# Values' second parts beside the first in the stationary operand: attention and stick-breaking weights streamed twice instead of three times

## The chip, the cores and the metric

The kernel runs on one core of one Trainium2 chip. The metric is the device time of one execution in microseconds (us), as a median over runs. Five engines matter: TensorE (PE; its loads of the stationary operand are PEld), VectorE (DVE), ScalarE (ACT), GpSimd (POOL), and SyncE (SP), which issues the DMAs.

## What is computed

Two layers of a hybrid trunk over 16 meta tokens and 512 frames, in float32. The first layer has eight heads of sparse attention (an indexer picks the keys) and four heads of gated linear attention; the second has four heads of retention and eight heads of stick-breaking attention. Cut to what the change touches:

```python
# attention, first layer: p is softmax over the chosen keys
return jnp.einsum('bhqk,bqkhd->bqhd', p, vg)
# stick-breaking, second layer
log_1m = jnp.where(ok, -jax.nn.softplus(z), 0.0)
after = lax.cumsum(log_1m, axis=3, reverse=True) - log_1m
w = jnp.where(ok, jnp.exp(jax.nn.log_sigmoid(z) + after), 0.0)
return jnp.einsum('bhqs,bshd->bqhd', w.astype(v.dtype), v)
...
oa = oa.reshape(bsz, P, -1) * jax.nn.silu(ag)
od = od.reshape(bsz, P, -1) * jax.nn.silu(dg)
```

In both, each of eight heads (64 wide) multiplies a matrix of weights, queries by keys, with the values, and the result is multiplied by its gate.

## The kernel before

A product of two float32 matrices is made of three matmuls in the chip's fp32r type: each operand is split into a first part (`hi`, a rounding copy on ScalarE) and a second part (`lo`, the rest, by a subtraction on VectorE), and first x first, second x first and first x second are summed in PSUM. The projections work so (`wh`, `wl` for the weights, `hh`, `hl` for the hidden state, accumulated in `acc`), and so do the sums of values here.

Heads go in pairs, p = 0 to 3 in each layer: `a0` to `a3` in the first (attention), `d0` to `d3` in the second (stick-breaking). `pair` runs a pair by a list of words. `S` makes scores of one head (odd = 0 or 1) for a unit of query blocks (u = 0: blocks 0 and 1; u = 1: blocks 2 and 3), `T` turns the finished weights by transposes into PSUM (`x`) and splits them into `pt` tiles, `M` does the same with the weights on the 16 meta keys (`ptm`), and `P` calls `weighted`, which multiplies the `pt` tiles (moving operand) with the values (stationary operand) into the PSUM tile `y`. There is one `y` buffer; the linear-attention and retention heads use it as well.

Before, one `y` tile of 128 rows x 512 queries belongs to a pair from its first `P` to its end: rows 0 to 63 for the even head, 64 to 127 for the odd one. So that one head's matmul leaves the other's rows alone, the values stand in tiles `vt` (`vh`, `vl`) with 64 zero columns beside each head, cleared on GpSimd: a stationary operand of 128 columns is one head's 64 and 64 zeros. Each key block takes three matmuls (first values x first weights, first x second, second x first), and a pair's end is one VectorE product of `y` with the gate `gt` into the mix `mx`.

The program is recorded first and then put in order by a list scheduler (`Recorder.order`), which gives each instruction a cost and a due time, and takes for each engine what is ready. Every engine then runs its list in that order; buffers of one kind are handed out in the order in which they are first used. All instructions are issued from line 406, so the profile tells them apart by tiles and shapes, not by lines. `out_ab` and `out_cd` are the out-projections; `out_ab` goes over the mix in the order 4, 5, 6, 7, 0, 1, 2, 3, the attention's last pair (`a3`, number 3) at the very end, each part split into `hh` and `hl` by `split_mix`. The first layer's order is `V G0 G1 D A0 A1 C0 C1 A2 A3 C2 C3` (C: the attention's gates), the second's `V S0 S1 R0 S2 S3 R1` (S: stick-breaking, R: retention heads).

## Time and profile before

| | |
|---|---|
| time, median of 3 runs | 653.55 us (652.32 to 654.64) |
| the profiled execution | 654.6 us, of which the span is 652.7 us |
| TensorE busy | 633.3 us (97%), 4469 matmuls |
| VectorE busy | 483.5 us (74%) |
| ScalarE busy | 406.3 us (62%) |
| GpSimd busy | 68.9 us (11%) |

Busy time is the union of an engine's instructions. Matmuls overlap in the engine, so a busy TensorE is not one at its peak, and the duration shown for one matmul is longer than the distance to the next. The profile follows the chain that ended last backward from the end, and says for each idle time which instruction ended it.

### The profile page before, as it was taken

To read this page: it belongs to the slowest core of one execution; us is meant where nothing else is said; L and a number is where in the kernel's file an instruction comes from. 1 tells how busy PE (TensorE), PEld (TensorE's weight loads), DVE (VectorE), ACT (ScalarE), POOL (GpSimd) and SP (SyncE) were. 2 spreads that over 40 slices of the span, in tenths; PEclk is the share of its full clock that TensorE was granted. 3 is DMA by queue.
4 is the path that set the end of the run, shared out by engine and by line. 5 is a ranking of instruction groups with operands and counts; after the bars stand their busy time and mean duration, and the time that the engine had idled before them with its cause. 6 is when DMAs were issued, how large, how long until landed. Compare 5 with 4: busy or idle time off the path is not lost.

```text
span 652.7 us, 12208 instructions
## 1 busy us (share of the span) xinstructions
PE 633.3 (97%) x4469; PEld 582.8 (89%) x4469; DVE 483.5 (74%) x1182; ACT 406.3 (62%) x912; POOL 68.9 (11%) x116
## 2 busy tenths in 40 slices
PE   7999999899999999999999999999999999999995
PEld 6979999898989999999899999888998888988884
DVE  6768799899977859779642674699945699966643
ACT  5656563362344868599643675799844699944434
POOL 4000100120010000001122110001200001110030
PEclk9899999799999999999999999999999999999998
DMA  8437223232322323112243272203322203235403
GB/s 245 111 83 230 66 66 83 58 90 52 80 66 77 89 66 99 50 49 66 65 132 115 65 238 87 66 17 98 82 83 65 77 5 98 65 98 157 150 17 129
DMA packets 91103, 59.25 MB, mean 91 GB/s; under 512 B 7314, under 2 KB 81628, under 8 KB 91044
## 3 DMA queue, kind: packets, MB, share of 16 engines
q1 hardware_dynamic: 91044, 58.48, 31.4%
q8 instruction: 35, 0.57, 0.3%
q14 instruction: 24, 0.20, 0.1%
HBM read 53.18 MB, written 6.90 MB: 92 GB/s over the span
## 4 chain that ended last, share of the span: by engine, by line
PE 78%; DVE 12%; ACT 8%; issue 2%; POOL 0%; DVEq 0%; ACTq 0%; POOLq 0%
PE acc L406 53%; PE x L406 17%; PE y L406 8%; ACT wt L406 4%; DVE st L406 2%; DVE wt L406 2%; DVE wl L406 2%; DVE lt L406 1%; ACT st L406 1%; DVE pt L406 1%; DVE m L406 1%; ACT wh L406 1%; DVE kl L406 1%; ACT ptm L406 1%; ACT pt L406 1%
## 5 line engine op out<-in xcount | busy, mean ns | idle before, releaser
L406 PE MATMUL acc<-hh,wh 128*128 128x272 f32 (+2 forms) x968 | 244.8, 314 | 1.4 <-DVE lt L406 0.4
L406 PE MATMUL acc<-hl,wh 128*128 128x272 f32 (+2 forms) x968 | 236.4, 305 | 0.9 <-DVE hl L406 0.9
L406 PE MATMUL acc<-hh,wl 128*128 128x272 f32 (+2 forms) x968 | 234.6, 303 | 2.1 <-DVE wl L406 2.1
L406 ACT ACTIVATE wh<-raw 128x512 fp32r<-128x512 f32 x154 | 96.1, 631 | 121.5 <-PE acc L406 107.7
L406 PEld LDWEIGHTS acc<-hh,wh 128*128 128x128 f32 x968 | 159.5, 190 | 8.5 <-issue 0.9
L406 PEld LDWEIGHTS acc<-hh,wl 128*128 128x128 f32 x968 | 158.5, 190 | 8.7 <-DVE wl L406 2.9
L406 PEld LDWEIGHTS acc<-hl,wh 128*128 128x128 f32 x968 | 158.6, 190 | 5.4 <-DVE hl L406 1.7
L406 DVE TENSOR_TENSOR wl<-raw,wh 128x512 fp32r<-128x512 f32 x154 | 109.7, 717 | 63.0 <-ACT wh L406 60.7
L406 ACT ACTIVATE wt<-x 128x272 f32<-128x272 f32 (+3 forms) x100 | 43.1, 454 | 24.4 <-PE x L406 15.7
L406 POOL TENSOR_TENSOR gt<-gt,wt 128x528 f32<-128x528 f32 (+1 forms) x16 | 21.7, 1355 | 331.0 <-ACT wt L406 309.7
L406 PE MATMUL x<-st,st 128*128 128x272 f32 (+6 forms) x240 | 50.9, 290 | 0.0
L406 PE MATMUL x<-ident,wt 128*128 128x128 f32 (+2 forms) x300 | 46.0, 274 | 2.0 <-DVE wt L406 1.2
L406 ACT ACTIVATE wt<-wt 128x528 f32<-128x528 f32 (+3 forms) x74 | 43.2, 606 | 3.9 <-DVE wt L406 3.3
L406 PEld LDWEIGHTS x<-st,st 128*128 128x128 f32 (+2 forms) x240 | 37.3, 185 | 7.1 <-ACT wt L406 2.5
L406 ACT ACTIVATE wt<-wt,tiny 128x272 f32<-128x272 f32 (+5 forms) x64 | 34.6, 562 | 9.3 <-DVE tiny L406 8.8
L406 PEld LDWEIGHTS x<-ident,wt 128*128 128x128 f32 (+2 forms) x300 | 34.5, 139 | 6.4 <-DVE pt L406 1.4
L406 PE MATMUL y<-pt,vt 128*128 128x256 f32 (+1 forms) x288 | 39.4, 279 | 0.2 <-DVE pt L406 0.2
L406 PEld LDWEIGHTS y<-pt,vt 128*128 128x128 f32 x288 | 36.6, 190 | 0.9 <-DVE pt L406 0.5
L406 ACT ACTIVATE st<-acc 64x528 fp32r<-64x528 f32 (+1 forms) x58 | 34.7, 599 | 1.0 <-DVE lt L406 0.4
L406 DVE TENSOR_TENSOR_SCAN wt<-wt,wt 128x64 f32<-128x64 f32 (+5 forms) x50 | 30.9, 657 | 2.1 <-ACT wt L406 1.7
L406 ACT ACTIVATE wt<-wt,one 128x528 f32<-128x528 f32 (+3 forms) x42 | 29.5, 704 | 0.2
L406 DVE TENSOR_TENSOR pt<-x,pt 128x384 fp32r<-128x384 f32 (+1 forms) x48 | 28.1, 596 | 1.8 <-ACT pt L406 0.9
(187 smaller groups left out, 884.6 us busy)
## 6 DMA issues: line engine op xcount, KB each, us to landing
raw<-in_w_in_ab_dram SPq DMA_DIRECT2D x64, 256.0 KB, 2.8
raw<-in_w_in_cd_dram SPq DMA_DIRECT2D x56, 256.0 KB, 2.9
raw<-in_w_out_ab_dram SPq DMA_DIRECT2D x16, 256.0 KB, 2.7
raw<-in_w_out_cd_dram SPq DMA_DIRECT2D x16, 256.0 KB, 2.6
rep<-rows SPq DMA_DIRECT2D x8, 328.0 KB, 6.2
lt<-rep SPq DMA_DIRECT2D x8, 264.0 KB, 3.0
pt<-in_x_dram SPq DMA_DIRECT2D x8, 256.0 KB, 4.9
wt<-in_x_dram SPq DMA_DIRECT2D x8, 256.0 KB, 3.1
```

The lines of the kernel that those rows point to most:

```text
L406: getattr(getattr(self.core, o.eng), o.name)(*[bind(x) for x in o.args], **{k: bind(x) for k, x in o.kw.items()})
```

## The change

The zeros go. A tile `vs` holds for each head its first part and its second part side by side, 128 columns, and these are the stationary operand: one pass of the weights' first part gives first x first on one half of the rows and second x first on the other, and a pass of the weights' second part adds to both (second x second comes with it). So each key block takes two matmuls instead of three. The two heads now share all 128 rows and stand in different columns: one `y` tile holds one unit, 256 queries, of both heads, and a pair takes it twice. The values of the meta keys keep their zeros in one tile `vm`; their matmul now runs twice for a unit, once for each head. What the passes leave in the two halves has to be added: `both_parts` copies for each head the half on the other rows to an SBUF tile `low` (ScalarE, 64 x 256) and adds the two halves into `mx` (VectorE, 64 x 256). The product with the gate then works on `mx` in place.

```diff
@@ -457,7 +457,7 @@
         return self.wk.tile([P, 512], dt, tag="pt", bufs=self.PT, name=self.name("pt"))
     def vt(self, dt=F32):
-        return self.wk.tile([P, 768], dt, tag="vt", bufs=8, name=self.name("vt"))
+        return self.wk.tile([P, 1024], dt, tag="vt", bufs=4, name=self.name("vt"))
     def lt(self, dt=F32):
         return self.wk.tile([P, T], dt, tag="lt", bufs=8, name=self.name("lt"))
@@ -968,11 +968,9 @@
         nc = self.nc
-        vh = [self.vt(F32R) for _ in range(NB)]
-        vl = [self.vt(F32R) for _ in range(NB)]
-        vm = self.wk.tile([96, 512], F32R, tag="vm", bufs=1, name=self.name("vm"))
-        for t in vh + vl:
-            nc.gpsimd.memset(t.rearrange("p (f c) -> p f c", f=4)[:, :, 64:128].bitcast(F32), 0.0)
+        vs = [self.vt(F32R) for _ in range(NB)]
+        vm = self.wk.tile([96, 768], F32R, tag="vm", bufs=1, name=self.name("vm"))
+        nc.gpsimd.memset(vm.rearrange("p (f c) -> p f c", f=4)[:, :, 64:128].bitcast(F32), 0.0)
         early = []
         if self.second:
@@ -992,10 +990,10 @@
                 a = self.project(src, col + P * f, self.hh, self.hl)
             v = self.wt()
             nc.scalar.copy(v, a)
-            self.add(self.value_steps(f, v, vh, vl, vm), self.LAG["v"], f"v{f}")
-        return vh, vl, vm
-
-    def value_steps(self, f, v, vh, vl, vm):
+            self.add(self.value_steps(f, v, vs, vm), self.LAG["v"], f"v{f}")
+        return vs, vm
+
+    def value_steps(self, f, v, vs, vm):
         nc = self.nc
         z = self.tiny([P, 2, NMETA])
         nc.gpsimd.memset(z, 0.0)
@@ -1004,22 +1002,23 @@
         t = self.tr()
         for b in range(NB):
             self.transpose(t[:, P * b:P * (b + 1)], v[:, blk(b)])
-        heads = lambda x: x[:, 192 * f:192 * f + 192].rearrange("p (o c) -> p o c", c=64)[:, 0:3:2, :]
         for b in range(NB):
             tb = t[:, P * b:P * (b + 1)].rearrange("p (o c) -> p o c", o=2)
-            self.hi(heads(vh[b]), tb)
-            self.lo(heads(vl[b]), tb, heads(vh[b]))
+            x = vs[b][:, 256 * f:256 * (f + 1)].rearrange("p (o c) -> p o c", c=64)
+            self.hi(x[:, 0:4:3, :], tb)
+            self.lo(x[:, 1:3, :], tb, x[:, 0:4:3, :])
         yield 1
-        c = slice(P * f, P * (f + 1))
+        c = lambda r: vm[r, 192 * f:192 * (f + 1)].rearrange("p (o c) -> p o c", c=64)[:, 0:3:2, :]
         t = self.tr()
         self.transpose(t[:32, :P], z.rearrange("p o c -> p (o c)"))
-        self.hi(vm[0:32, c], t[:32, :P])
-        self.hi(vm[32:64, c], t[:32, :P])
-        self.lo(vm[64:96, c], t[:32, :P], vm[0:32, c])
+        tv = t[:32, :P].rearrange("p (o c) -> p o c", o=2)
+        self.hi(c(slice(0, 32)), tv)
+        self.hi(c(slice(32, 64)), tv)
+        self.lo(c(slice(64, 96)), tv, c(slice(0, 32)))
         yield 1
-    def vcols(self, t, p, odd):
-        return t[:, 192 * p + 64 * odd:192 * p + 64 * odd + P]
+    def meta_values(self, vm, p, odd):
+        return vm[:, 192 * p + 64 * odd:192 * p + 64 * odd + P]
     def weights_meta(self, pm, g):
@@ -1054,18 +1053,31 @@
             at += P * nb
         return parts
-    def weighted(self, o, parts, v, p, odd, first, last):
-        nc = self.nc
-        vh, vl, vm = v
-        if first is not None:
-            c = slice(2 * P * first, 2 * P * (first + 1))
-            nc.tensor.matmul(o[:, c], vm[:, P * p:P * (p + 1)], self.ptm[:, c], start=True, stop=False)
+    def weighted(self, o, parts, v, p, odd, u):
+
+
+        nc = self.nc
+        vs, vm = v
+        for h in (0, 1) if odd == 0 else ():
+            nc.tensor.matmul(o[:, 256 * h:256 * (h + 1)], self.meta_values(vm, p, h),
+                             self.ptm[:, 256 * u:256 * (u + 1)], start=h == 0, stop=False, skip_group_check=True)
         for i, (j, b0, nb, ph, pl) in enumerate(parts):
-            dst = o[:, P * b0:P * (b0 + nb)]
-            xh, xl = self.vcols(vh[j], p, odd), self.vcols(vl[j], p, odd)
-            nc.tensor.matmul(dst, xh, ph, start=False, stop=False)
-            nc.tensor.matmul(dst, xh, pl, start=False, stop=False)
-            nc.tensor.matmul(dst, xl, ph, start=False, stop=last and i == len(parts) - 1)
+            at = 256 * odd + P * (b0 - 2 * u)
+            x = vs[j][:, 256 * p + P * odd:256 * p + P * (odd + 1)]
+            for k, w in enumerate((ph, pl)):
+                nc.tensor.matmul(o[:, at:at + P * nb], x, w, start=False, stop=k == 1 and i == len(parts) - 1,
+                                 skip_group_check=True)
+
+    def both_parts(self, o, tmp, u):
+        nc = self.nc
+        c = slice(NMETA + 256 * u, NMETA + 256 * (u + 1))
+        t = self.wk.tile([P, 256], F32, tag="low", bufs=2, name=self.name("low"))
+        for h in range(2):
+            r, q = slice(64 * h, 64 * h + 64), slice(64 - 64 * h, 128 - 64 * h)
+            nc.scalar.copy(t[r], o[q, 256 * h:256 * (h + 1)])
+        for h in range(2):
+            r = slice(64 * h, 64 * h + 64)
+            nc.vector.tensor_tensor(tmp[r, c], o[r, 256 * h:256 * (h + 1)], t[r], op=ALU.add)
     def pair(self, scores, pm, v, p, gates, tmp, lag, meta=None):
@@ -1092,15 +1104,17 @@
                     del ws[odd, b]
             elif word[0] == "P":
                 yield from self.wait(at[odd, u])
-                if o is None:
+                if odd == 0:
                     o = self.pv()
-                self.weighted(o, turned.pop((odd, u)), v, p, odd, u if odd == 0 else None, odd == 1)
+                self.weighted(o, turned.pop((odd, u)), v, p, odd, u)
+                if odd:
+                    self.both_parts(o, tmp, u)
                 yield 1
             elif word[0] == "L" and meta:
                 yield from meta(odd)
         while not gates:
             yield 1
-        self.nc.vector.tensor_tensor(tmp[:, NMETA:], o, gates[0][:, NMETA:], op=ALU.mult)
+        self.nc.vector.tensor_tensor(tmp[:, NMETA:], tmp[:, NMETA:], gates[0][:, NMETA:], op=ALU.mult)
         if meta:
             yield from meta(2)
@@ -1220,7 +1234,8 @@
                 mm.append(pmm)
             else:
                 t = self.tr()
-                nc.tensor.matmul(t[:, :NMETA], v[2][:, P * p:P * (p + 1)], mm[0], start=True, stop=True)
+                for h in range(2):
+                    nc.tensor.matmul(t[:, :NMETA], self.meta_values(v[1], p, h), mm[0], start=h == 0, stop=h == 1)
                 nc.vector.tensor_tensor(tmp[:, :NMETA], t[:, :NMETA], gates[0][:, :NMETA], op=ALU.mult)
             yield 1
         yield from self.pair(scores, pm, v, p, gates, tmp, self.LAG["a"], meta)
```

The scheduler puts many instructions elsewhere. Three places follow.

ScalarE, end of the first layer. Before, around the last three first parts of a3's turned weights (`pt` from `x`; `pmm` are the meta queries' own weights, `wt` from `x` is the residual being turned):

```order
L406 ACTIVATE pt_4484<-x_4472 128x384
L406 ACTIVATE pt_4493<-x_4480 128x512
L406 ACTIVATE pt_4503<-x_4495 128x384
L406 ACTIVATE pmm_4527<-x_4519 32x16 x2
L406 COPY wt_4560<-x_4546 128x512
L406 ACTIVATE hh_4193<-mx_1939 128x528
```

The same place now:

```order
L406 ACTIVATE pt_4458<-x_4441 128x384
L406 ACTIVATE hh_4165<-mx_1929 128x528
L406 ACTIVATE pt_4472<-x_4461 128x512
L406 ACTIVATE pt_4487<-x_4469 128x384
L406 ACTIVATE pmm_4522<-x_4518 32x16 x2
L406 COPY low_4525<-y_4477 64x256 x2
L406 COPY wt_4543<-x_4531 128x512
L406 COPY wt_4543<-x_4541 128x16
L406 ACTIVATE hh_4165<-mx_1929 128x528
```

The first `hh` here is a2's split, which has moved in between a3's weights; the last is a3's, and two copies of `y` stand ahead of it.

VectorE, the same place. Before, from the last of a3's second parts to the split of its mix:

```order
L406 TENSOR_TENSOR pt_4510<-x_4495,pt_4503 128x384
L406 TENSOR_TENSOR pmm_4527<-x_4519,pmm_4527 32x16
L406 TENSOR_TENSOR mx_1939<-y_4399,gt_4228 128x512
L406 TENSOR_TENSOR mx_1939<-x_4544,gt_4228 128x16
L406 TENSOR_TENSOR hl_4206<-mx_1939,hh_4193 128x528
```

And now:

```order
L406 TENSOR_TENSOR pt_4494<-x_4469,pt_4487 128x384
L406 TENSOR_TENSOR tiny_4090<-tiny_4090,tiny_4408 16x32
L406 TENSOR_TENSOR wl_4501<-raw_3965,wh_4381 128x512
L406 TENSOR_TENSOR pmm_4522<-x_4518,pmm_4522 32x16
L406 TENSOR_TENSOR mx_1929<-y_4477,low_4525 64x256 x2
L406 TENSOR_TENSOR mx_1929<-x_4528,gt_4214 128x16
L406 TENSOR_TENSOR mx_1929<-mx_1929,gt_4214 128x512
L406 TENSOR_TENSOR hl_4179<-mx_1929,hh_4165 128x528
```

Two adds out of `y` have come in ahead of the product with the gate, which no longer reads `y`.

ScalarE, second layer, from d1's last scores to its last turned weights (`wh` are splits of weight matrices, `wt` from `acc` is a projection on its way to the retention head). Before:

```order
L406 ACTIVATE wt_6338<-x_6302 128x256
L406 ACTIVATE wt_6353<-acc_6172 128x528
L406 ACTIVATE wt_6238<-wt_6238 128x528
L406 ACTIVATE wh_6370<-raw_6078 128x512
L406 ACTIVATE wh_6382<-raw_6088 128x512
L406 ACTIVATE pt_6390<-x_6376 128x512
L406 ACTIVATE wh_6398<-raw_6099 128x512
L406 ACTIVATE wt_6338<-wt_6338 128x528
L406 ACTIVATE pt_6415<-x_6400 128x384
```

And now:

```order
L406 COPY low_6331<-y_6263 64x256 x2
L406 ACTIVATE wh_6340<-raw_6032 128x512
L406 ACTIVATE wt_6346<-acc_6154 128x528
L406 ACTIVATE wh_6353<-raw_6054 128x512
L406 ACTIVATE wh_6362<-raw_6090 128x512
L406 ACTIVATE wh_6371<-raw_6119 128x512
L406 ACTIVATE wt_6209<-wt_6209 128x528
L406 ACTIVATE wt_6175<-wt_6175 128x400
L406 ACTIVATE wt_6319<-wt_6319 128x528
L406 COPY wt_6397<-acc_6303 128x528
L406 ACTIVATE wh_6406<-raw_6291 128x512
L406 ACTIVATE pt_6418<-x_6395 128x512
```

The first of d1's last `pt` tiles now stands behind five weight splits where two stood before it, and the projections that use these splits have moved ahead with them.

## Rows read from the trace of the kernel before

**Rows 1.** The page, part 1: busy us, share of span, instructions.

```profile
PE 633.3 (97%) x4469; PEld 582.8 (89%) x4469; DVE 483.5 (74%) x1182; ACT 406.3 (62%) x912; POOL 68.9 (11%) x116
```

**Rows 2.** The page, part 4: the chain that ended last, by engine.

```profile
PE 78%; DVE 12%; ACT 8%; issue 2%; POOL 0%; DVEq 0%; ACTq 0%; POOLq 0%
```

**Rows 3.** Groups by form: busy us, mean ns | idle before them.

```profile
L406 PE MATMUL y<-pt,vt 128*128 128x256 f32 x192 | 31.6, 288 | 0.2 <-DVE pt L406 0.2
...
L406 PE MATMUL y<-pt,vt 128*128 128x128 f32 x96 | 14.5, 260 | 0.0
...
L406 DVE TENSOR_TENSOR mx<-y,gt 128x512 f32<-128x512 f32 x8 | 5.5, 687 | 4.1 <-PE y L406 3.4 <-PE x L406 0.7
...
L406 POOL MEMSET vt<- 128x256 f32 x16 | 4.3, 310 | 12.1 <-PE y L406 12.0
```

**Rows 4.** Timeline of TensorE, 471 to 475: start us, us, instructions.

```profile
471.46 2.93 PE L406 MATMUL y<-pt,vt 128*128 128x256 f32 x24
474.22 0.45 PE L406 MATMUL acc<-hh,wh 128*128 128x512 f32 x1
```

**Rows 5.** The chain in order of time, second layer: start us, us, what.

```profile
471.50 2.88 PE y L406 x25
...
519.77 3.67 ACT wt L406 x9
```

**Rows 6.** Windows, second layer: length, busy us of each engine, clock, DMA.

```profile
420.00:470.00 50.00, 48.83 (x338) 44.04 (x338) 46.97 (x100) 48.72 (x109) 4.15 (x4) 1.00 0.20 55
...
445.00:450.00 5.00, 5.00 (x31) 4.30 (x30) 3.95 (x11) 4.00 (x8) 1.30 (x1) 1.00 0.70 201
...
460.00:465.00 5.00, 5.00 (x44) 4.99 (x43) 4.96 (x11) 5.00 (x13) 1.51 (x1) 1.00 0.11 27
...
470.00:475.00 5.00, 5.00 (x37) 4.56 (x36) 4.88 (x9) 1.18 (x4) 2.33 (x3) 1.00 0.55 157
475.00:480.00 5.00, 5.00 (x31) 4.01 (x29) 1.51 (x3) 3.67 (x10) 0.00 (x0) 1.00 0.52 150
```

**Rows 7.** Windows, first layer: PE, PEld, DVE, ACT, POOL busy.

```profile
280.00:310.00 30.00, 29.59 (x241) 28.89 (x240) 25.54 (x95) 29.30 (x73) 3.20 (x6) 1.00 0.18 54
...
305.00:310.00 5.00, 4.59 (x39) 4.36 (x38) 4.94 (x17) 4.96 (x13) 1.88 (x5) 1.00 0.02 3
```

**Rows 8.** The chain in order of time, 305 to 307.

```profile
305.00 0.63 DVE hl L406
...
305.67 1.24 PE acc L406 x8
```

**Rows 9.** Timeline, end of the first layer.

```profile
321.73 1.26 PE L406 MATMUL y<-pt,vt 128*128 128x256 f32 x9
...
323.10 0.69 DVE L406 TENSOR_TENSOR mx<-y,gt 128x512 f32<-128x512 f32 x1 [0.70 <-PE x L406]
...
323.71 0.16 DVE L406 TENSOR_TENSOR mx<-x,gt 128x16 f32<-128x16 f32 x1
...
324.08 0.65 ACT L406 ACTIVATE hh<-mx 128x528 fp32r<-128x528 f32 x1
```

**Rows 10.** The chain, late second layer, projections of 512 columns.

```profile
601.77 8.58 PE acc L406 x37
```

**Rows 11.** Groups by form nearest to the new copies, adds and products.

```profile
L406 ACT ACTIVATE ptm<-x 32x256 fp32r<-32x256 f32 x32 | 11.8, 368 | 1.7 <-PE x L406 1.4
...
L406 ACT ACTIVATE wt<-x 128x256 f32<-128x256 f32 x24 | 9.7, 404 | 4.0 <-PE x L406 3.9
...
L406 DVE SCALAR_TENSOR_TENSOR st<-acc,wt 64x256 f32<-64x256 f32 x16 | 6.7, 420 | 0.2
...
L406 DVE TENSOR_TENSOR st<-st,wt 128x512 f32<-128x512 f32 x2 | 1.4, 684 | 0.0
```

**Rows 12.** The chain in order of time, first layer, behind a0's matmuls.

```profile
242.07 1.35 PE y L406 x12
...
265.59 0.70 DVE pt L406
```

## Prediction

> **What bounds the kernel now.** I began with the page. TensorE is busy for 97% of the span, VectorE for 74%, ScalarE for 62% [rows 1], and the chain that ended last stands on TensorE for 78% of the span, on VectorE for 12% and on ScalarE for 8% [rows 2]. So a matmul that goes away is worth its time, as long as TensorE, and not one of the two others, ends the wait behind it. The groups by form then show what the change cuts: the matmuls of turned weights with values, 192 of 256 columns and 96 of 128 columns [rows 3]. Their mean of 288 ns is the length of one in the pipeline, not what it costs: in the timeline 24 of them start at 471.46 and the next projection at 474.22, so 2.76 / 24 = 0.115 us each, whether 256 or 128 wide [rows 4].
>
> Then I asked stage by stage which engine is full. The cut matmuls lie in eight heads' pairs: a0 to a3 in the first layer, whose last y matmuls end just before 323 [rows 9], and d0 to d3 in the second, two side by side at a time. In the second layer the chain runs over TensorE from the first pair's y matmuls past the second's, the 25 at 471.50 included, up to 519.77, where ScalarE takes over [rows 5]. But the windows say that this stretch has no room elsewhere: VectorE and ScalarE are busy for 4.96 and 5.00 of 5 us at 460 to 465, and over the 50 us from 420 ScalarE rests 1.3 us in all; room comes back only from 470 on ScalarE and from 475 on VectorE [rows 6]. In the first layer ScalarE is full too: 29.30 of the 30 us from 280 to 310, with VectorE at 25.54; at 305 to 310 both are at 4.94 or more of 5 and TensorE falls to 4.59 [rows 7]. There the chain is held by VectorE and not by TensorE before the projections at 305.67 [rows 8]. At the end of this layer everything stands in a row: last y matmuls, gate product, split, out-projection [rows 9].
>
> **The change part by part.** *Removed and added on TensorE.* Before, one pair issues 36 matmuls of three kinds and 2 of the meta keys: 38. After, 24 and 4: 28. Over eight pairs 80 fewer, 80 x 0.115 = 9.2 us. Four matmuls for the meta queries' own rows come on top, at most 4 x 0.115 = 0.5. So TensorE has at most 8.7 us less: 4.1 in the first layer, 4.6 in the second.
>
> The Trainium skill ("TensorE: Matmul & The Clock Gate", Back-to-back issue gap) gives a sustained spacing of 81 ns at 128 columns and 131 ns at 512; by it the 80 matmuls would be worth, as an estimate, 6.5 to 10.5 us. The trace differs from it on the wide side: 37 projection matmuls of 512 columns take 8.58 us, 232 ns each [rows 10], so I go by the 0.115 of this stream.
>
> *The drain.* Each pair now drains its bank twice, each time with two ScalarE copies of 64x256 out of PSUM and two VectorE adds of 64x256. No such copy is in the trace; the nearest rows are 32x256 at 0.368 and 128x256 at 0.404 us on ScalarE, so time goes by columns and not by partitions, and I take 0.37. The add is nearest to the 64x256 rows out of PSUM, 0.420 [rows 11]. Over 32 of each: 11.8 us (to 12.9) more ScalarE, 13.4 us more VectorE. The gate product then reads SBUF instead of PSUM: 0.687 before [rows 3], 0.684 for a product of that shape in SBUF [rows 11]; nothing.
>
> In the program both adds stand behind both copies of their bank. The Trainium skill ("PSUM — Partial Sum Buffer", PSUM bank collisions raise a hardware error) says that two engines may not touch the same bank and quadrant at once, reads included, so this is not slack that a better order could win back. No run here shows it. The drain costs 2 x 0.37 + 2 x 0.42 = 1.6 us in a row; with the first add beside the second copy it would be 1.2.
>
> *Values and memsets.* The splits of the values are as many and as large. The 16 clearings of value tiles on GpSimd (0.310 each [rows 3]) go; GpSimd is busy 11% [rows 1] and nothing on the chain waits for it, so 0. The order of the first 25 us shifts by a few rows on VectorE; I put 0 on it, and 0.4 us either way in the range.
>
> *Second layer, d0 to d3.* Two pairs stand side by side, twice. Each time 20 matmuls go, 2.3 us on a stretch where TensorE carries the chain. Against it ScalarE gets 8 x 0.37 = 3.0 and VectorE 8 x 0.42 = 3.4 us. Six of these eight fall before the second pair's last weights, 2.2 and 2.5 us, and the main gap there is 445 to 450 with 1.0 us on each [rows 6]. So those weights come 1.2 to 1.5 us late, more by the order, in which three more weight splits stand ahead of them. What is late next is the second pair's last y matmuls. TensorE has projections of the next retention head to do meanwhile, and the order has put more of them ahead of these y's; ScalarE's idle 3.8 us at 470 to 475 and VectorE's 3.5 at 475 to 480 take up the backlog. I take 1.6 of 2.3 as kept, 3.2 of 4.6 for the layer. Ends: all 4.6; or a loss, see the second rival.
>
> *First layer, a0 and a1.* 20 matmuls, 2.3 us. Some lie on TensorE's part of the chain, as the 12 at 242.07 do for a0; but behind them the chain passes to VectorE (the turned weights at 265.59 [rows 12]), which gains work, so I keep half: 1.2.
>
> *a2 and a3.* Six of their eight drains' copies fall into ScalarE's full stretch: 2.2 us less the 0.7 of idle time left between 280 and 310 [rows 7] makes it 1.5 longer, and the matmuls saved here turn into waiting. Then the end of the layer: from the last y matmul (321.73 and 9 matmuls, to 322.99) to the split at 324.08 it is now 1.1 us [rows 9]; after, 1.6 of drain, 0.69 of product, 0.17 of the small one and some 0.1 of handing over, 2.5: 1.4 longer. Seven matmuls fewer ahead of it give back 0.8, and the split of a2, which the order now puts among the turning copies of a3, adds its 0.65 [rows 9]. Together 1.2 lost. No cover: the residual's transposes are all that TensorE has there, before and after.
>
> *Sum.* -3.2 - 1.2 + 1.5 + 1.2 = -1.7 us. The profiled execution took 654.6 us (span 652.7 and 1.9 around it), 1.05 over the median of the runs; 654.6 - 1.7 = 652.9, and less the 1.05: 651.9.
>
> **The rivals.** *The saving arrives nearly whole.* For it: TensorE is the bound in 78% of the chain, the order pulls projections forward as cover, and the work of ScalarE and VectorE is 62% and 74% of the span [rows 1]. Against it: the full windows above, exactly where the matmuls lie. With 2.3 kept each time in the second layer, 2.3 in a0 and a1, and 1.0 lost at the end of the first: -5.9, 647.6; all 8.7 with no loss would be 644.9.
>
> *ScalarE becomes the bound in the second layer: slower.* Place: 420 to 470 and its repeat. ScalarE's own work there grows by up to 3.0 us against 1.3 us of idle time [rows 6]; if TensorE runs out of projections and waits for the second pair's last weights, each repeat ends 1.7 later instead of 1.6 earlier: +3.4, and with the first layer's +1.5 it is +4.9, 658.5; half as bad 656. It decides once the wait at those y matmuls exceeds the 2.3 us saved. For it: the full windows. Against it: the room behind 470, where the next retention heads need little of both engines.
>
> *The matmuls were hidden anyway.* Then only drains and tail remain, +1.5 to +2.7: 655.5. TensorE's unbroken chain in the second layer speaks against it; I count it with the slower ones.
>
> **How the numbers follow.** About 0.3% (2 us) is what a measurement of this kernel tells from no change. My forecast, part kept and part given back: 0.50, with a range of its own from 650.0 to 653.7. Nearly whole: 0.22, around 648. The slower ones: 0.28, around 656. From the first I count 0.21 as faster by over 0.3% (below 651.6) and 0.29 as within; from the second 0.21 and 0.01; from the third 0.21 slower and 0.07 within. So faster 0.42, same 0.37, slower 0.21. The range leaves out a tenth on either side: 647.5 to 656.5.
>
> **What would show it.** Right: 80 fewer y matmuls at 0.115 us spacing; copies of 64x256 near 0.37 and adds near 0.42 us; ScalarE about 418 us busy, VectorE about 497; the wait from the last y of a3 to the split of its mix at 2.5 us instead of 1.1; the second layer's two stretches from the first score to the next retention head each some 1.6 us shorter. Wrong: TensorE waiting for ScalarE at d1's and d3's last y matmuls (rival two), or the first layer as short as the second (rival one); a price of the drain well off 1.6.

## The result and the profile after

The changed kernel takes 659.35 us (median of 9 runs, 656.18 to 662.34) where the kernel before takes 654.37 (9 runs beside them): a ratio of 1.0082, 95% interval 1.006 to 1.0104. It is slower by some 5 us; the forecast was 651.9. The profiled execution took 658.0 us, span 656.1. Runs of one kernel differ with the mean granted clock of the run: in 24 runs of the kernel before, 652.0 to 652.5 us at 0.991 to 0.992 and 653.0 to 654.7 at 0.985 to 0.989.

The page of the changed kernel, part 1, the chain by engine, and the group of the `y` matmuls:

```profile
PE 628.5 (96%) x4393; PEld 574.4 (88%) x4393; DVE 497.3 (76%) x1214; ACT 418.7 (64%) x944; POOL 64.8 (10%) x102
...
PE 57%; DVE 21%; ACT 17%; issue 3%; DMA 1%; SPq 0%; DVEq 0%; ACTq 0%
...
L406 PE MATMUL y<-pt,vt 128*128 128x256 f32 x192 | 29.2, 279 | 0.4 <-DVE pt L406 0.2
```

The change did to the engines what its diff says: 76 matmuls fewer [rows 1], the two `y` groups of [rows 3] down from 288 matmuls to 192 (the page gives both widths under one), ScalarE 12.4 us busier and VectorE 13.8. What moved is the chain that ended last: TensorE held 78% of it [rows 2], now 57%; VectorE and ScalarE hold 38% together, where they held 20%.

The drain's instructions by tile (duration min/median/max in ns, first and last start):

```profile
L406 ACT COPY low<-y x32: 357/366/371, 228.9 to 582.6; 64x256 f32<-64x256 f32 x32
L406 DVE TENSOR_TENSOR mx<-y,low x32: 397/422/430, 230.7 to 583.7; 64x256 f32<-64x256 f32 x32
```

The chain of the changed kernel through the second layer's first two pairs (start us, us, what):

```profile
423.00 2.01 ACT wt L406 x5
...
432.27 4.27 ACT wt L406 x10
...
436.57 0.37 ACT low L406
...
436.95 0.36 ACT low L406
...
454.58 0.37 ACT low L406
...
456.34 0.38 ACT low L406
...
457.98 0.44 DVE wt L406
...
465.25 6.01 DVE wt L406 x6
...
471.42 0.33 DVE mx L406
...
471.88 1.05 PE x L406 x8
...
476.99 1.77 PE y L406 x15
```

Before, the chain left the two other engines at 437.58 and was TensorE's from there up to 519.77 [rows 5]; the chain of the kernel before at that place:

```profile
436.94 0.61 DVE wl L406
...
437.58 0.73 PE acc L406 x2
```

Now it runs over ScalarE from 420 to 458, four of the new copies in it, then over VectorE to 471.8. The second pair's last `y` matmuls start at 476.99 instead of 471.50; of these 5.5 us, 2.9 were there before the layer began (the table below), and 2.6 are the pair's own. TensorE does not wait at these matmuls themselves but ahead of them, for VectorE, at two places of each repeat where neither the kernel before nor the one without drains (no_drain) waits; the first repeat's:

```profile
441.61 0.50 PE L406 MATMUL acc<-hh,wl 128*128 128x512 f32 x1 [0.45 <-DVE wl L406]
...
471.88 0.28 PE L406 MATMUL x<-ident,pm 128*32 128x128 f32 x1 [0.89 <-DVE pm L406]
```

Three places of its timeline, in order of time: the front of the program, the end of the first layer, and the first of `d1`'s two drains with what stands around it on ScalarE and VectorE (start us, us, instructions; in brackets the idle time before and what ended it):

```profile
117.73 1.29 POOL L406 TENSOR_TENSOR gt<-gt,wt 128x528 f32<-128x528 f32 x1 [16.91 <-ACT wt L406]
117.80 1.77 DVE L406 TENSOR_TENSOR wl<-raw,wh 128x512 fp32r<-128x512 f32 x1
120.79 0.22 PE L406 MATMUL x<-ident,st 64*16 64x64 f32 x1 [2.88 <-DVE attm L406]
...
323.02 0.44 PE L406 MATMUL y<-pt,vt 128*128 128x128 f32 x2
323.51 0.74 ACT L406 COPY low<-y 64x256 f32<-64x256 f32 x2
324.29 0.86 DVE L406 TENSOR_TENSOR mx<-y,low 64x256 f32<-64x256 f32 x2 [0.60 <-ACT low L406]
325.27 0.68 DVE L406 TENSOR_TENSOR mx<-mx,gt 128x512 f32<-128x512 f32 x1
325.98 0.64 ACT L406 ACTIVATE hh<-mx 128x528 fp32r<-128x528 f32 x1 [0.61 <-DVE mx L406]
...
465.16 4.39 DVE L406 TENSOR_TENSOR_SCAN wt<-wt,wt 128x528 f32<-128x528 f32 x3
...
467.10 0.74 ACT L406 COPY low<-y 64x256 f32<-64x256 f32 x2
...
469.47 1.78 DVE L406 TENSOR_TENSOR wt<-wt,wt 128x528 f32<-128x528 f32 x3
...
471.33 0.41 DVE L406 TENSOR_TENSOR mx<-y,low 64x256 f32<-64x256 f32 x1
```

At the end of the first layer the drain stands in a row, 323.46 (last `y` matmul) to 325.98: 2.5 us where it was 1.1 [rows 9]. In the second layer the copies of 467.10 are done at 467.84, but their adds stand behind three scans and three subtractions on VectorE, up to 471.33. The rows at 117 to 121 the prediction had not looked at; they come below.

**Where the time went, by marks.** Five instructions on VectorE stand at the same place of the work in every kernel here: the fourth `wt<-y,tiny` (the last linear-attention head, 201.48 in the kernel before), the last `lt<-acc,wt` of 128x256 (the hidden state behind the first layer, 369.17), the first and third `tiny<-y` (the retention heads behind `d0`, `d1` at 487.64 and behind `d2`, `d3` at 589.10), and the span's end. Their shift against the kernel before, and the difference from mark to mark, is what a stage gained or lost in one profiled execution:

| profiled execution | front, to 201 | first layer, to 369 | d0, d1, to 488 | d2, d3, to 589 | end in all |
|---|---|---|---|---|---|
| changed kernel | +0.5 | +2.4 | +0.3 | +0.1 | +3.4 |
| no_drain | +1.8 | -2.2 | -2.5 | -2.6 | -5.4 |
| copies_only | +2.5 | -2.0 | -1.0 | -1.2 | -1.6 |
| vector_only | +1.6 | -0.7 | -1.1 | -1.2 | -1.3 |
| before_drain | -1.7 | +3.5 | +1.5 | +1.5 | +4.8 |
| a3_end | +2.8 | +2.4 | +0.2 | +0.2 | +5.6 |
| whole_copy | +3.2 | +1.0 | -0.6 | -0.8 | +2.7 |
| drain_layer2 | +1.7 | -2.1 | +0.2 | +1.1 | +0.8 |
| gpsimd_second | +3.2 | +2.1 | +0.4 | +0.2 | +5.8 |
| vector_first | -1.1 | +1.3 | +0.3 | +0.1 | +0.5 |
| whole_copy_vector_first | +1.3 | +0.9 | -0.5 | -0.9 | +0.7 |
| before_gpsimd_copy | -2.5 | 0.0 | 0.0 | 0.0 | -2.5 |
| second_layer_only | -2.3 | 0.0 | -0.9 | -1.0 | -4.2 |

The profiled execution of the kernel before is itself 1.05 over its median, and its front has a stretch of fallen clock (0.95, 0.50 and 0.70 of full speed between 116 and 128) that others of the same front lack. So the first column holds chance as well: before_gpsimd_copy, which differs from the kernel before by one small copy, stands at -2.5 there. The first layer's column holds a stretch of fallen clock at its end in the changed kernel, a3_end, whole_copy, gpsimd_second and whole_copy_vector_first, and the column `d2`, `d3` one in drain_layer2; for the rest the columns behind the front repeat, in kernels of the same order, within 0.1. The other rows are the experiments, which follow. The scheduler sorts each variant anew: against the kernel that it was made from, TensorE's list differs in 41 places (a3_end) to 128 (no_drain), so what a variant costs has its new order in it. Only the three with a GpSimd copy and nothing else against their model (gpsimd_second, vector_first, before_gpsimd_copy), and whole_copy_vector_first against whole_copy, keep every other engine's list as it was.

### The profile page after: what moved, and what is told of

Same layout as the page of the kernel before. It is cut to its first block, busy times and chain, and to the rows that moved or that the text cites. A ratio compares the mean times of both kernels' runs of the same rounds, so it can differ in the third digit from the quotient of the medians.

```text
span 656.1 us, 12102 instructions
## 1 busy us (share of the span) xinstructions
PE 628.5 (96%) x4393; PEld 574.4 (88%) x4393; DVE 497.3 (76%) x1214; ACT 418.7 (64%) x944; POOL 64.8 (10%) x102
## 4 chain that ended last, share of the span: by engine, by line
PE 57%; DVE 21%; ACT 17%; issue 3%; DMA 1%; SPq 0%; DVEq 0%; ACTq 0%
PE acc L406 39%; PE x L406 13%; ACT wt L406 9%; DVE wt L406 5%; PE y L406 4%; DVE st L406 3%; DVE wl L406 3%; ACT st L406 3%; DVE lt L406 2%; DVE m L406 2%; DVE pt L406 1%; ACT wh L406 1%; ACT pt L406 1%; DMA pt<-in_x_dram 1%; DVE mx L406 1%
## 5 line engine op out<-in xcount | busy, mean ns | idle before, releaser
L406 ACT ACTIVATE wt<-wt 128x400 f32<-128x400 f32 (+3 forms) x74 | 43.5, 603 | 4.1 <-DVE wt L406 3.3
L406 DVE TENSOR_TENSOR_SCAN wt<-wt,wt 128x64 f32<-128x64 f32 (+5 forms) x50 | 32.4, 699 | 0.2
L406 PE MATMUL y<-pt,vt 128*128 128x256 f32 x192 | 29.2, 279 | 0.4 <-DVE pt L406 0.2
L406 PEld LDWEIGHTS y<-pt,vt 128*128 128x128 f32 x192 | 25.6, 189 | 2.2 <-DVE pt L406 2.1
```

The lines of the kernel that those rows point to most:

```text
L406: getattr(getattr(self.core, o.eng), o.name)(*[bind(x) for x in o.args], **{k: bind(x) for k, x in o.kw.items()})
```

## The experiments

The names are those of the table. **1 to 4: which engine's part of the drain costs, and where.** In no_drain:

```diff
-                    self.both_parts(o, tmp, u)
+                    pass
...
-        self.nc.vector.tensor_tensor(tmp[:, NMETA:], tmp[:, NMETA:], gates[0][:, NMETA:], op=ALU.mult)
+        self.nc.vector.tensor_tensor(tmp[:, NMETA:], o, gates[0][:, NMETA:], op=ALU.mult)
```

In copies_only the two ScalarE copies go straight into the mix and nothing is added; in vector_only two VectorE copies do so:

```diff
+            nc.scalar.copy(tmp[r, c], o[r, 256 * h:256 * (h + 1)])
...
+            nc.vector.tensor_copy(tmp[r, c], o[r, 256 * h:256 * (h + 1)])
```

In before_drain the kernel before has the copies and adds behind each second head's `P`, into a tile that nothing reads:

```diff
+                if odd:
+                    self.both_parts(o, u)
```

> The changed kernel without the drain: no copies, no adds, the gate product reads the bank of the pair's second unit as before the change. It leaves out the adding of the halves and the first unit of each pair. Theory (the saving on TensorE is real and the drain's 11.8 us on ScalarE and 13.4 us on VectorE eat it): 5 to 8.7 us under the kernel before, 646 to 649. Rival A (the matmuls were hidden anyway): within 2 us of before. Rival B (the new order and two turns of the one y buffer cost the time): still above before, 656 or more.

> The drain on ScalarE alone: its two copies of 64x256 write the mix, and no adds follow; the other halves are left out. Theory with ScalarE as the engine that decides: near the changed kernel, 656 to 659. Theory with VectorE as the one: near the kernel without drain, 647 to 650. Both share: about 652.

> The drain on VectorE alone: two copies of 64x256 out of the bank in place of the adds, no work on ScalarE; the other halves are left out. Mirror of the run with ScalarE alone: 647 to 650 if ScalarE decides, 656 to 659 if VectorE does, about 652 if both share.

> The kernel before with the drain put on top, its result unused: two ScalarE copies and two VectorE adds of 64x256 behind each unit, all matmuls as before. Theory: the drain by itself costs what the change lost plus what TensorE saved, 8 to 12 us, so 662 to 666. Rivals A and B: the drain is off the path, at most 2 us more than before.

Measured, with the kernel before at 653.05 on the same chip: no drain 649.01 (ratio 0.9942, 0.992 to 0.9964); copies only 651.81 (0.9976, 0.996 to 0.9992); VectorE only 653.08 (0.9993, 0.9978 to 1.0008); the kernel before with the drain on top 659.5 (1.0105, 1.0087 to 1.0123).

The first three lie where sharing engines would put them, no drain at the very edge of its 646 to 649; the fourth missed its 662 to 666, and its rivals' 2 us as well.

What follows, by the table's columns. The matmuls' saving is real where nothing is paid for it: 2.2, 2.5 and 2.6, 7.2 of the 8.7 forecast (in the time only 3.8 of it shows, since its front is later, as 8 to 11 tell). In each repeat of the second layer the ScalarE copies cost 1.5 and 1.4, VectorE's part 1.4 and 1.4 (its copies take the 0.422 of the adds); their sum, 2.9 and 2.8, is what the whole drain costs there (2.8 and 2.7, the changed kernel against no drain). So both halves of the drain stand on the path, and they take the saving away to within 0.3 us. TensorE shows where: in a repeat it has the same matmuls with and without the drain (803 in the first, 639 in the second), but its idle time is 2.7 us with it, 1.2 without, 1.8 with the copies alone and 1.5 to 1.6 with VectorE's part alone; the rest of the 2.8 lies in wider spacing that the trace counts as busy. In the first layer the parts cost 0.2 and 1.5, but together 4.6, of which 1.1 is a fallen clock (vector_first, without it, is at +1.3 there, so 3.5): there they line up. On the kernel before, the same drain costs 3.5 in the first layer too, with its clock up, but only 1.5 per repeat of the second instead of 2.8. One reading is that TensorE's matmuls, still all there, cover part of it; another, that nothing reads its result, so that nobody waits for the adds. The runs do not part the two.

**5: the last drain of the first layer.**

```diff
-                if odd:
+                if odd and not (meta and p == 3 and u == 1):
                     self.both_parts(o, tmp, u)
...
+            self.nc.vector.tensor_tensor(tmp[:, NMETA + 256:], o[:, 256:], g[:, NMETA + 256:], op=ALU.mult)
```

> The changed kernel with one of its sixteen drains gone, the one at the very end of the first layer (a3's second unit): the gate product takes these 256 columns straight from the bank, so the halves of that unit are not added. Theory (the loss sits in a few places): this drain stands in a row with everything else and lets TensorE rest long enough that its granted clock falls at 324 to 332, so both go: 1.4 us of drain and about 1.2 of clock, near 656.0 where the changed kernel would be 658.4 on a chip that runs the kernel before in 653.05 (ratio about 1.0045). Rival (each of the sixteen drains costs the same, 10.3 us between the changed kernel with and without drains, 0.64 each): 657.8, and the clock at 324 to 332 is no part of it.

Measured 657.05 (ratio 1.007, 1.0044 to 1.0095), between the two. In its profiled execution the first layer costs +2.4 as in the changed kernel, and the clock falls all the same, only earlier. Windows of this kernel (length, busy us of PE, PEld, DVE, ACT, POOL, granted clock, DMA):

```profile
316.00:320.00 4.00, 2.62 (x23) 2.36 (x22) 3.85 (x17) 3.71 (x9) 0.00 (x0) 1.00 0.06 17
320.00:324.00 4.00, 3.09 (x15) 2.55 (x16) 3.87 (x11) 3.20 (x8) 0.00 (x0) 0.65 0.38 114
324.00:328.00 4.00, 3.54 (x26) 3.24 (x25) 1.53 (x4) 0.35 (x2) 0.00 (x0) 0.92 0.22 66
```

VectorE and ScalarE are nearly full up to 320, and TensorE is busy for 2.62 of 4 us there. That the drain in a row at the very end is what costs is not borne out: the theory missed, and its 1.4 us did not come. That the work ahead of the tail, on the two full engines, comes late as well would explain it, but this variant has an order of its own, so it is not shown. The interval doesn't exclude a gain of a microsecond.

**6: one wide copy instead of two narrow ones.**

```diff
-        t = self.wk.tile([P, 256], F32, tag="low", bufs=2, name=self.name("low"))
+        t = self.wk.tile([P, 512], F32, tag="low", bufs=2, name=self.name("low"))
+        nc.scalar.copy(t, o)
...
-            nc.scalar.copy(t[r], o[q, 256 * h:256 * (h + 1)])
...
-            nc.vector.tensor_tensor(tmp[r, c], o[r, 256 * h:256 * (h + 1)], t[r], op=ALU.add)
+            nc.vector.tensor_tensor(tmp[r, c], o[r, 256 * h:256 * (h + 1)], t[q, 256 * h:256 * (h + 1)], op=ALU.add)
```

> The changed kernel whole, with another drain: one ScalarE copy of the whole bank, 128x512, in place of two of 64x256; the adds then read the copy from the other half's partitions. By the rows of 128x512 copies (0.59 us) against two of 0.37 ScalarE gains 0.15 us per drain, 2.4 over sixteen, and one instruction less stands ahead of the adds. Theory: ScalarE's part of the second layer's chain shrinks by 4 x 0.15 in each repeat and the first layer's end by 0.15, about 1 us in all: near 657.4. Rival (VectorE's queue alone sets the second layer, since the adds stand behind its scans): no change, 658.4.

Measured 654.87 (ratio 1.0026, 1.0012 to 1.004): 3.7 us less by the ratios, not 1. Its copies, by tile:

```profile
L406 ACT COPY low<-y x16: 580/588/648, 231.6 to 580.7; 128x512 f32<-128x512 f32 x16
```

0.588 against 2 x 0.366, as the theory had it, so ScalarE gains 2.3 us; but all of it and more comes back in time, 1.4 in the first layer (clock fallen at its end in both) and 0.9 in each repeat. That fits a ScalarE queue that is the chain with the adds waiting behind it; how much of it is the new order is not parted. With this drain the second layer does gain.

**7: do the layers pay on their own?**

```diff
-                if odd:
+                if odd and not meta:
                     self.both_parts(o, tmp, u)
```

> The changed kernel with drains in the second layer only; in the first layer the gate products take the banks as they stand, so the halves are not added there. Theory: the two layers pay on their own. From the mark at 212 us on, the first layer ends 2.2 us earlier than in the kernel before, as without drains, and each repeat of the second layer still loses the saving, +0.4 and +0.1: near 654.0, and no fallen clock at 324 to 332. Rival (the second layer loses because the first hands it over late): each repeat gains 2.4 as without drains, near 649.5.

Measured 654.86 (ratio 1.0018, 1.0004 to 1.0032). Yes: the first layer gains 2.1 as without any drain, and the first repeat still loses its saving (+0.2). The second repeat is at +1.1, with a stretch of fallen clock at 540 to 544 that the others don't have there; why is open. The second layer's loss does not come from a late first layer.

**8 to 11: the front.** In eight profiles of the change's front (the changed kernel, no_drain, copies_only, vector_only, a3_end, whole_copy, drain_layer2, gpsimd_second) TensorE's wait at 119 to 121 is 2.9 us; in the kernel before and before_drain it is 1.7. The kernel before there, timeline:

```profile
117.33 0.68 DVE L406 TENSOR_TENSOR wl<-raw,wh 128x512 fp32r<-128x512 f32 x1
117.36 1.80 POOL L406 TENSOR_TENSOR gt<-gt,wt 128x528 f32<-128x528 f32 x1 [16.99 <-ACT wt L406]
119.22 0.22 PE L406 MATMUL x<-ident,st 64*16 64x64 f32 x1 [1.68 <-DVE attm L406]
```

Two instructions that both read two tiles from SBUF come within 0.1 us of each other. Before, VectorE's subtraction is first and takes 0.68, and GpSimd's product is stretched from 1.29 to 1.80. After, VectorE's list is 0.1 us later against GpSimd's, the product is first, and the subtraction is stretched to 1.77; the two `m` of VectorE, the masked copy `attm` and TensorE's matmul wait behind it. (In before_drain the two records start 0.01 us apart the other way round; the durations, 0.67 and 1.83, tell who went first.) The Trainium skill ("SBUF — State Buffer", Who interferes with whom) says that a VectorE instruction with two SBUF inputs contends with a GpSimd instruction that reads SBUF, that the port pair they share is an exclusive lock, and that issue order decides who blocks. The trace agrees in both directions: after, the subtraction is longer by 1.09 of the 1.22 us for which the product still ran beside it; before, the product by 0.51 of 0.65. To undo it, a small GpSimd copy is put ahead of the first gate product: in gpsimd_second to a tile of its own (first line), in the three others in place, on the product's operand (second):

```diff
+            nc.gpsimd.tensor_copy(z, e[:64, :16])
...
+            nc.gpsimd.tensor_copy(e[:64, c][:, :16], e[:64, c][:, :16])
         nc.gpsimd.tensor_tensor(t[:, c], t[:, c], e[:, c], op=ALU.mult)
```

> The changed kernel whole, with one small GpSimd copy (64x16) ahead of its first gate product at 117.7 us, nothing else moved on any engine. In the changed kernel and in all three of its variants so far, VectorE's subtraction of a weight's halves (128x512) starts 0.03 to 0.07 us after GpSimd's product there and takes 1.77 to 1.80 us; in the kernel before and in the one with drains on top of it, it starts 0.01 to 0.03 us ahead of the product and takes 0.68. TensorE then waits 2.9 us in place of 1.7, and the granted clock falls behind it in four of four profiles against one of two. Theory (this is a cost of the change that has nothing to do with its drains or matmuls): the copy lets VectorE go first, its subtraction takes 0.68 and TensorE waits 1.7, so 1.2 us less, and up to 3 where the clock stays up: 655.4 to 657.2. Rival (the front of the program costs nothing, the loss is all drains): 658.4.

Measured 659.99 (ratio 1.0092, 1.0073 to 1.0111). The list scheduler had put the copy behind the product, which decides nothing; the subtraction still took 1.79 and the wait 2.88. So this is the changed kernel once more, and says nothing on the theory.

> The changed kernel whole, with a GpSimd copy of 64x16 in place, on the very tile that the first gate product at 117.7 us reads, so that the product can't go ahead of it; nothing else moves on any engine. (The copy of the run before it stood behind the product in the program and so changed nothing.) Theory (the front of the program is part of the price: the product starts ahead of VectorE's subtraction of a weight and holds it up): now the subtraction goes first, takes some 0.7 to 1.0 us in place of 1.78, TensorE waits 1.7 to 2.0 us there in place of 2.9, and where its granted clock stays up behind it, up to 2 us more come back: 656.3 to 658.3, where the changed kernel is at 658.4 to 659.5. Rival (this stall is taken up later, and only drains cost): 658.4 to 659.5.

> The kernel with one 128x512 copy per drain, which ran at 654.87, with the same GpSimd copy ahead of the first gate product. Theory as for the changed kernel with that copy: 1.0 to 3 us less, 652 to 653.9, level with the kernel before (653.1). Rival (the front costs nothing): 654.9.

> The kernel before with the same GpSimd copy ahead of its first gate product, as a control. There VectorE's subtraction already starts 0.03 us ahead of the product. Theory: nothing to win, 653.1, within 0.5. Rival (a later product is worth something by itself, or it was a coin toss from run to run in this kernel too): 651 to 652.5.

Measured, with the kernel before at 652.87: vector_first 656.43 (ratio 1.0057, 1.0035 to 1.0079), whole_copy_vector_first 653.64 (1.0009, 0.9996 to 1.0022), the kernel before with the copy 652.8 (0.9999, 0.9986 to 1.0011). The timeline of vector_first:

```profile
117.24 0.19 POOL L406 COPY wt<-wt 64x16 f32<-64x16 f32 x1 [16.90 <-ACT wt L406]
117.31 0.67 DVE L406 TENSOR_TENSOR wl<-raw,wh 128x512 fp32r<-128x512 f32 x1
117.51 1.63 POOL L406 TENSOR_TENSOR gt<-gt,wt 128x528 f32<-128x528 f32 x1
119.20 0.22 PE L406 MATMUL x<-ident,st 64*16 64x64 f32 x1 [1.79 <-DVE attm L406]
```

The order on every other engine is the same row for row, the subtraction is back at 0.67 and the wait at 1.79. By the ratios 1.6 us come back against the changed kernel's runs, 2.3 against those of gpsimd_second, and 1.1 with the whole copy; the intervals overlap, so the size is known to about a microsecond, while the mechanism shows in the rows. Since the order is the same, one instruction can be followed through the three programs: TensorE's matmul behind the wait (above, 119.20 in vector_first and 120.79 in the changed kernel), and ScalarE's `wt<-y` behind the stretch in which the clock may fall. In vector_first, in the changed kernel and in gpsimd_second:

```profile
128.82 0.49 PE L406 MATMUL y<-st,st 128*128 128x128 f32 x2 [0.82 <-DVE st L406]
...
129.34 0.60 ACT L406 ACTIVATE wt<-y 128x512 f32<-128x512 f32 x1 [3.34 <-PE y L406]
```

```profile
130.94 0.60 ACT L406 ACTIVATE wt<-y 128x512 f32<-128x512 f32 x1 [2.27 <-PE y L406]
```

```profile
121.08 0.27 PE L406 MATMUL x<-ident,st 64*16 64x64 f32 x1 [2.88 <-DVE attm L406]
...
133.61 0.60 ACT L406 ACTIVATE wt<-y 128x512 f32<-128x512 f32 x1 [2.34 <-PE y L406]
```

The changed kernel is 1.59 late at the matmul (0.5 of it from before 116 us, 1.1 from the collision) and 1.60 at `wt<-y`: its fallen clock (0.84 and 0.73, at the end of this document) cost nothing in the end. Between the two instructions TensorE is idle for 1.0 us in vector_first (0.82 of it in the first of these rows) and not at all in the two others, so the slow stretch went in part into waits that were there anyway. In gpsimd_second the clock stays down longer (0.50, 0.50 and 0.73 from 120 to 132), and 1.88 becomes 4.27: 2.4 us. Where VectorE was first anyway, the same copy brings nothing, as expected.

**12: the change where it pays.** The kernel before in the first layer, the change with the whole copy in the second alone (`fold` marks the second layer's values, `folded` is the changed `weighted`, and `meta` is there in the first layer only):

```diff
+        fold = src == "w_in_cd"
...
+                if not meta:
+                    self.folded(o, turned.pop((odd, u)), v, p, odd, u)
+                    if odd:
+                        self.both_parts(o, tmp, u)
+                    yield 1
+                    continue
```

> The kernel before in the first layer, word for word, and the change in the second layer alone, with the drain of one 128x512 copy; whole. Theory (three places, each on its own): the front and the first layer are those of the kernel before and cost nothing, and the second layer's two repeats gain what they gained in the profile of the kernel with one copy per drain, 0.6 and 0.8: 651.5 where the kernel before is at 652.9, ratio 0.998. Rival (that kernel's second layer was short only since its first layer handed it over late): 652.9, no change.

Measured 650.49 (12 runs, 650.0 to 654.03; ratio 0.9974, 0.9958 to 0.999), the kernel before 652.58 beside it. This version beats both. Page and copies by tile:

```profile
PE 626.7 (97%) x4429; PEld 574.9 (89%) x4429; DVE 489.9 (76%) x1198; ACT 409.9 (63%) x920; POOL 67.7 (10%) x112
```

```profile
L406 ACT COPY low<-y x8: 580/594/642, 431.2 to 573.9; 128x512 f32<-128x512 f32 x8
```

Front and first layer are the kernel before's but for one pair of instructions in another order near 227 us, and the repeats gain 0.9 and 1.0 of the 2.5 that the matmuls are worth there. Its interval excludes no change, and the rival with it.

## Why the prediction was wrong, point by point

- **TensorE's saving, at most 8.7: right.** Without drains 7.2 arrive, about evenly in the three places (no_drain). The 0.115 of one matmul is a mean: by their single starts in that row the wide ones go at 0.12 and the narrow ones at 0.095.
- **The drain's prices: right.** Copies 0.366 (taken 0.37), adds 0.422 (0.42), ScalarE 418.7 and VectorE 497.3 us busy (418 and 497).
- **Second layer, "I take 1.6 of 2.3 as kept": this step failed.** Nothing is kept: +0.3 and +0.1 instead of -1.6 each. I let ScalarE's room at 470 to 475 and VectorE's at 475 to 480 [rows 6] take up the backlog, but that room lies behind the work that the second pair's last weights wait for. The queues ahead of it were full, and each of the drain's parts costs about half of its busy time, 1.4 to 1.5 of 2.9 and of 3.4; the projections put ahead are no cover, since TensorE's idle time in a repeat grows by the 1.5 us told above. Rival two had the mechanism, ScalarE and then VectorE as the chain, but not the size, breaking even instead of losing 1.7 each time, and not the place: TensorE waits for VectorE ahead of the last turned weights, not for ScalarE at the last `y` matmuls.
- **First layer, -1.2 + 1.5 + 1.2 = +1.5: right in sum, short of the clock.** vector_first, whose clock stays at 1.00 there, shows +1.3; the changed kernel's profile +2.4, with the clock at 0.94 and 0.63 from 324 to 332. The tail takes 2.5 us as forecast. That the tail by itself is worth 1.2 is not shown (a3_end), so the parts are unproven and the sum may be right by luck. The fallen clock, 1.1, was in no term.
- **"Values and memsets: 0": this step failed too, unseen.** I put the shift of the first 25 us' order at 0 with 0.4 either way. At 117 VectorE is 0.1 us later against GpSimd than before (what moved it was not followed), and it loses the ports to a GpSimd product that by my words nothing on the chain waits for. That costs 1.1 us of waiting, and behind it nothing (the changed kernel) to 2.4 us (gpsimd_second) of clock; by the times, 1.1 to 2.3 us.
- **The sum.** In vector_first, which takes the collision away, the profile is 3.0 us longer than in before_gpsimd_copy: 1.3 first layer, 0.4 second, 1.3 front. Against second_layer_only, whose front is the kernel before's, this last part is 1.2, of which 0.3 is there at the first weight's split on ScalarE (9 us), 0.5 comes by 25 us and 0.3 between 178 and 200; it was not followed further and stays open. Chance may be in it: the kernel before and before_gpsimd_copy, of one order up to there, are 1.0 apart at 26 us. The changed kernel's profile is 2.8 longer than vector_first's: 0.5 by 116 us, 1.1 by the collision and 1.1 by the clock at the end of the first layer. Its median run is 1.3 longer still, at a lower mean clock (0.979 against 0.986). So the result stands near rival two's 658.5 for other reasons than rival two's.
- **Rival three (the matmuls were hidden anyway): out**, by no_drain. **Rival one (nearly whole)** failed by the drain, and no version with the wide copy reaches it: the best of them gains 0.26%.

## What to carry to other kernels

When work moves from the full engine to two others, price it by the stretch where it lands: if their queues have no room ahead of the next thing that the first engine waits for, room behind it is worth nothing (that the time saved on the first engine was part of the cover is likely, but not shown). One wide instruction for two narrow ones can then be worth more than its busy time, here 3.2 us by the marks for 2.3, and the change may pay in one stage only, so measure stages by marks and keep it there. After any reordering, look for a VectorE and a GpSimd instruction with SBUF operands that start within a tenth of a microsecond: which is first may have flipped far from the edit, and the one that lost shows no idle time, only a longer record.

## What the runs showed of the hardware that was not expected

**The clock behind a wait.** Windows of 4 us, the changed kernel first, behind its wait of 2.9 us at 120 and at the end of its first layer, then vector_first (waits 1.8 us at 119):

```profile
120.00:124.00 4.00, 3.21 (x18) 2.54 (x19) 3.96 (x14) 0.90 (x2) 0.00 (x0) 0.84 0.25 66
124.00:128.00 4.00, 4.00 (x27) 4.00 (x26) 3.71 (x11) 0.95 (x3) 0.00 (x0) 0.73 0.27 68
...
324.00:328.00 4.00, 2.97 (x19) 2.25 (x19) 2.32 (x5) 2.11 (x6) 0.31 (x1) 0.94 0.14 42
328.00:332.00 4.00, 4.00 (x22) 3.77 (x22) 2.61 (x4) 2.44 (x4) 0.98 (x1) 0.63 0.42 125
```

```profile
120.00:124.00 4.00, 4.00 (x31) 3.41 (x30) 3.87 (x11) 0.90 (x2) 0.00 (x0) 1.00 0.06 18
124.00:128.00 4.00, 3.83 (x31) 3.43 (x29) 3.71 (x12) 1.49 (x4) 0.00 (x0) 1.00 0.30 70
324.00:328.00 4.00, 3.23 (x22) 2.55 (x21) 2.43 (x5) 2.86 (x7) 0.00 (x0) 1.00 0.45 132
328.00:332.00 4.00, 4.00 (x35) 4.00 (x35) 1.79 (x3) 1.21 (x3) 1.63 (x1) 1.00 0.47 137
```

A window at 0.50 is one at 1.2 GHz, one at 1.00 at 2.4, and one between holds both. Behind the wait of 2.9 us the clock fell in eight profiles of eight; behind the same wait of 1.7 to 1.8 us in three of six (the kernel before, before_gpsimd_copy and whole_copy_vector_first, not in before_drain, vector_first and second_layer_only). Where the first layer has its drains (in a3_end all but the last), the clock fell at its end in five profiles of seven (not in before_drain and vector_first), and in none of the seven others. So a wait of a microsecond more can cost a second one behind it, and by chance: the first layer of vector_first, the same program but for one GpSimd copy far ahead, is 1.1 us shorter than that of the changed kernel. And a fall need not cost what it looks like: behind the wait at 120 it cost nothing in the changed kernel and 2.4 us in gpsimd_second.
